# The first token block's plain tiles ahead of the second weight's block products, and its norm beside them

## The chip, the core and the metric

The kernel runs on one core of a Trainium2 chip. TensorE multiplies, VectorE and ScalarE work on elements, GpSimd (POOL) helps VectorE, and SyncE (SP) issues most transfers between DRAM and the on-chip memory. TensorE's results arrive in eight banks of 512 columns of fp32 (b0 to b7 in the rows). The metric is the time of one execution in microseconds (us), as the device reports it; lower is better.

## What is computed

One layer of a streaming encoder on 1088 tokens (1024 of a prompt, 64 of a running stream), width 1024, hidden width 2816:

```python
def _layer_norm(x, g, b):
    mu = x32.mean(-1, keepdims=True)
    var = jnp.square(x32 - mu).mean(-1, keepdims=True)
    return (x32 - mu) * lax.rsqrt(var + LN_EPS) * g + b

def _swiglu(x, wi, wo):
    a, u = jnp.split(x @ wi, 2, axis=-1)
    return (jax.nn.silu(a) * u) @ wo

h = _layer_norm(alpha * x + 0.5 * _swiglu(x, ffn1_wi, ffn1_wo), ln1_g, ln1_b)
oa, ob, ga, gb, states = mixer(h)          # z = h @ w_in, top-k attention with an indexer, band attention
mix = (jax.nn.sigmoid(ga) * ya + jax.nn.sigmoid(gb) * yb) @ w_out
h = _layer_norm(alpha * h + mix, ln2_g, ln2_b)
h = _layer_norm(alpha * h + 0.5 * _swiglu(h, ffn2_wi, ffn2_wo), ln3_g, ln3_b)
```

## The kernel before

Everything is fp32. An operand is split into a head and a rest, and a product is three matmuls: head with head, head with rest, rest with head. Data lie transposed: 8 tiles of 128 of the width (d or k), 22 hidden tiles of 128 (f), tokens along the columns. Tokens are cut twice: into blocks b of 384, 384 and 320 for the plain products and norms (`TB`), and into halves of 544 (`HT`), of two pieces of 272 (`SUB`) each, for the products by blocks.

**Order of the work.** `Plan` simulates all engines with a cost for each instruction while the program is written. TensorE's stream is written out in order; the other engines' work is put in as tasks with dependencies and priorities, and whenever TensorE's simulated clock passes a task's start, the task is written into its engine's queue. Tasks for TensorE (a norm's three matmul steps) come in at that point too, so the order on each engine is fixed when the program is built and isn't changed on the chip. While `st["solo"]` is set GpSimd gets no tasks. All instructions are recorded by one helper; so they all have line L120, and are told apart by tile.

**An FFN** is built by `add_ffn7`, for FFN1 (`gi` 0) and FFN2 (`gi` 2). The first weight's products are done in a scheme of seven block products. Of the hidden tiles, 0 to 17 (`KEPT_OUT` = 18) go out to DRAM and come back as tiles a, which are split into factors `fac`. The second weight is applied to these 18 in seven block products over 9 pairs, in the order P2, P1, P6, P5, P3, P7, P4 (`second`); each of the 63 units is 24 matmuls of 272 columns into eight banks (272 of the 512 columns are used), and after a product's ninth pair `take_out` adds the banks to the outputs y on VectorE. P2, P1 and P3 concern half 0 of the tokens, the others half 1. Hidden tiles 18 to 21 are multiplied plainly (`out_products`): six matmuls of 384 or 320 columns for two hidden tiles, one output tile d and one block b, and a VectorE instruction adds the bank to y. `early` does tiles 18 and 19 for d = 0, 1 and all blocks ahead of the block products (36 matmuls), `last_outputs` does the others behind them (252), block by block. The weights come through units: a raw chunk of 128 x 512 arrives (`wr` or `q`), ScalarE makes its head and VectorE its rest in a half of a tile `w_s`, in a rotation of four halves.

**The norms.** `add_up` adds the eight y of a block into `acc` while its outputs come. `layer_norm(b)`, called after block b, then consists of: a matmul of `acc` with ones (mean); eight centrings; eight squares, summed into `lns`; matmuls of `lns` with ones (variance, 1 column); the root on ScalarE and the reciprocal on VectorE (`rstd`); matmuls with `ident` that spread it over the partitions; eight scalings; and the output by `put`. In FFN1 `put` also splits the result into the tiles x that the projection z multiplies. In this text LN(b) is this norm of block b. In FFN1 LN(0) runs beside block 1's products, LN(1) beside block 2's and z's, LN(2) beside z's. In FFN2 the last block has its own form (`last_norm`), which sums most of the columns ahead (`sq`, `rest`).

The last part of z's first stretch makes the indexer's keys and queries, KH and QI. `split(hi, lo, src)` makes their heads by a ScalarE copy and their rests by a VectorE subtraction, both written directly into the queues.

Of the kernel before, what the change touches and what calls it, by code (L numbers as in the profile page):

```python
# [32 lines left out]
P = 128  # L33
# [306 lines left out]
def tile_trunk(ctx, tc, a):  # L340
# [12 lines left out]
    roles, turn = {}, {}  # L353

    def bank(role):
        banks = roles[role]
        i = turn.get(role, 0)
        turn[role] = i + 1
        t = banks[i % len(banks)]
        return psp.tile([P, 512], F32, name=f"b{t}", tag=f"b{t}")  # L360
# [180 lines left out]
    def layer_norm(b, Y, ACC, gi, tmp, put, room=None):  # L541
# [11 lines left out]
        t_mean = plan.task("pe", f"ln{b}", mean, [summed[b]], 1, ln_free, when=lambda: ln_free()[0])  # L553

        def copy(y):
            nc.scalar.activation(room[:, 0, :n], z[y][:, :n], AF.Copy)
            give(z[y])
# [42 lines left out]
        def var():  # L600
            p = take()
            for j, (c, m) in enumerate(toks):
                nc.tensor.matmul(p[:m, j:j + 1], z["s", 0][:, c:c + m], ones[:, :1], start=True, stop=True)
# [3 lines left out]
        def root():  # L607
# [3 lines left out]
            give(z["v"])  # L611
# [9 lines left out]
        t_var = plan.task("pe", f"ln{b}", var, [t_sum], 1, ln_free, when=lambda: ln_free()[0])  # L621
        t_root = plan.task("act", f"ln_r{b}", root, [t_var], 1)
        t_inv = plan.task("dve", f"ln_i{b}", inv, [t_root], 1)
        t_bc = plan.task("pe", f"ln{b}", spread, [t_inv], 1, ln_free, when=lambda: ln_free()[0])
# [8 lines left out]
        for k in range(KT):  # L633
            if room is None:
                t1 = plan.task("dve", f"ln_n{b}", lambda k=k: scale(k), [t_bc], 3)
            else:
# [188 lines left out]
    def add_up(ACC, Y, d, b, n, tmp):  # L825
# [6 lines left out]
        if d:  # L832
            summed[b] = plan.task(adders(n), "acc", add, [summed[b]] if d > 1 else (), 2, None, [Y[d, b]])
# [55 lines left out]
    def add_ffn7(wi, wo, wl, G, gi, put, beside_it, last, end):  # L889
# [10 lines left out]
        at, low, F, ACC, Y = Bag(), {}, {}, {}, {}  # L900
# [259 lines left out]
        def early():  # L1160

            f0 = KEPT_OUT
            wait(*(F[f].t[x, s] for f in (f0, f0 + 1) for x in ("h1", "h2") for s in range(2)))
# [1472 lines left out]
```

## Time and profile before

| | us |
|---|---|
| median of 3 runs | 2483.65 (2481.89 to 2483.95) |
| the profiled execution | 2481.9 |
| its span | 2480.1 |
| TensorE busy in the span | 2418.6 (98%) |
| VectorE busy | 1752.4 (71%) |
| ScalarE busy | 1298.7 (52%) |
| GpSimd busy | 343.8 (14%) |
| mean granted TensorE clock | 0.987 |

The profile shows one execution. A share of busy time is an average over parts of the program with different limits, so it says which engine bounds the whole and not what a certain place waits for. Windows cut the span into stretches and give each engine's busy time in them, and the clock that TensorE was granted (1.00 is its higher level of 2.4 GHz, 0.50 the lower of 1.2). The view in order of time gives, for an engine, runs of alike instructions, the idle time before each run, and the instruction that ended it. Starts in it count from the span's start. Some places: the first weight of FFN1 ends and the second begins at 492, P7 runs from 635.5 to 662.5, P4 to 689.5, the plain products to 733.5, then z; in FFN2 the second weight begins at 2200, and P7 and P4 run from 2345.5 to 2399.5.

### The profile page before, as it was taken

How to read it: one execution, taken by the hardware profiler on the slowest of the kernel's cores; microseconds unless marked ns; L12 is line 12 of the kernel's file. 1: busy time of each engine (PE TensorE's matmuls, PEld its weight loads, DVE VectorE, ACT ScalarE, POOL GpSimd, SP SyncE). 2: the span in 40 equal slices, each digit the busy share in tenths (PEclk: the TensorE clock that was granted, in tenths of full speed). 3: DMA queues.
4: the chain of work that ended last, by engine and by line, in shares of the span. 5: the costliest groups of instructions: out<-in, count | busy, mean ns of one | idle time of the engine just before them, and what ended most of it. 6: DMA issues, size and time to landing. Idle time of an engine off the chain costs nothing.

```text
span 2480.1 us, 46835 instructions
## 1 busy us (share of the span) xinstructions
PE 2418.6 (98%) x17338; PEld 2379.3 (96%) x17338; DVE 1752.4 (71%) x4244; ACT 1298.7 (52%) x2736; POOL 343.8 (14%) x459
## 2 busy tenths in 40 slices
PE   9999999999998999999999999999999999999996
PEld 8999999999998999999999998999999999999995
DVE  7666655667675889898776667679856655657758
ACT  5333333343334698878857777446533333334324
POOL 0000000000044222122253332311000000000004
PEclk9999999999998999999999999999999999999997
DMA  5466532263222322332221112555256643145322
GB/s 185 125 208 200 175 104 87 83 217 102 82 81 84 122 74 76 96 96 89 67 82 60 57 42 68 181 190 171 87 164 191 191 126 92 61 140 185 94 64 73
DMA packets 222357, 289.61 MB, mean 117 GB/s; under 512 B 20832, under 2 KB 146640, under 8 KB 222096
## 3 DMA queue, kind: packets, MB, share of 16 engines
q1 hardware_dynamic: 216080, 279.71, 36.4%
q10 hardware_dynamic: 5488, 4.70, 0.7%
q8 instruction: 136, 2.23, 0.4%
q0 software_dynamic: 560, 2.21, 0.2%
q14 instruction: 93, 0.76, 0.1%
HBM read 211.81 MB, written 75.00 MB: 116 GB/s over the span
## 4 chain that ended last, share of the span: by engine, by line
PE 84%; DVE 8%; DMA 2%; ACT 2%; issue 1%; POOL 1%; SPq 0%; DVEq 0%; ACTq 0%; POOLq 0%
PE b L120 84%; DVE y L120 1%; DVE w L120 1%; DVE scores L120 1%; DVE pt L120 1%; DMA ff_d<-c 1%; DVE w_s L120 0%; DVE mk L120 0%; DVE k L120 0%; DVE x L120 0%; DVE sc L120 0%; DMA st<-in_wo_dram 0%; ACT scores L120 0%; SPq L120 0%; DMA a<-ff_d 0%
## 5 line engine op out<-in xcount | busy, mean ns | idle before, releaser
L120 PE MATMUL b<-x,w_s 128*128 128x384 f32 (+1 forms) x3528 | 637.5, 332 | 7.7 <-DVE x L120 4.6
L120 PE MATMUL b<-A,w_s 128*128 128x272 f32 (+1 forms) x4824 | 632.2, 291 | 5.5 <-ACT w_s L120 2.3
L120 PEld LDWEIGHTS b<-A,w_s 128*128 128x128 f32 x4824 | 619.4, 189 | 9.3 <-ACT A L120 2.6
L120 PEld LDWEIGHTS b<-x,w_s 128*128 128x128 f32 x3528 | 587.1, 189 | 15.4 <-DVE x L120 6.4
L120 PE MATMUL b<-S,w_s 128*128 128x272 f32 x4032 | 516.8, 288 | 2.6 <-ACT c L120 2.6
L120 PEld LDWEIGHTS b<-S,w_s 128*128 128x128 f32 x4032 | 509.0, 188 | 5.6 <-ACT c L120 3.9
L120 ACT ACTIVATE w_s<-wr 128x512 fp32r<-128x512 f32 (+1 forms) x359 | 243.6, 679 | 358.4 <-PE b L120 197.6
L120 DVE TENSOR_TENSOR w_s<-wr,w_s 128x512 fp32r<-128x512 f32 (+1 forms) x335 | 245.3, 735 | 139.9 <-ACT w_s L120 135.1
L120 PE MATMUL b<-fac,w_s 128*128 128x272 f32 x1800 | 228.2, 288 | 1.3 <-DVE y L120 1.3
L120 PEld LDWEIGHTS b<-fac,w_s 128*128 128x128 f32 x1800 | 226.8, 188 | 1.5 <-ACT fac L120 1.5
L120 POOL TENSOR_TENSOR w_s<-wr,w_s 128x256 fp32r<-128x256 f32 x180 | 139.9, 805 | 321.7 <-ACT w_s L120 114.1
L120 ACT ACTIVATE c<-b 128x272 f32<-128x272 f32 (+1 forms) x262 | 102.1, 391 | 98.3 <-PE b L120 87.6
L120 DVE TENSOR_TENSOR c<-c,b 128x272 f32<-128x272 f32 x240 | 103.5, 434 | 62.9 <-PE b L120 59.1
L120 DVE TENSOR_TENSOR pt<-b,pt 128x512 fp32r<-128x512 f32 (+4 forms) x184 | 96.1, 545 | 22.6 <-ACT pt L120 21.0
L120 ACT ACTIVATE c<-c 128x272 f32<-128x272 f32 x160 | 68.8, 432 | 77.5 <-DVE c L120 75.0
L120 ACT ACTIVATE w<-w,mx 128x640 f32<-128x640 f32 (+5 forms) x144 | 100.4, 699 | 15.4 <-DVE mx L120 14.2
L120 POOL TENSOR_TENSOR w_i<-wr,w_i 128x256 fp32r<-128x256 f32 (+1 forms) x9 | 8.2, 928 | 693.0 <-ACT w_i L120 693.0
L120 ACT ACTIVATE fac<-a 128x544 fp32r<-128x544 f32 x73 | 48.0, 657 | 104.6 <-PE b L120 86.5
L120 PE MATMUL b<-pt,v 128*128 128x256 f32 (+3 forms) x672 | 97.5, 276 | 4.1 <-DVE o L120 2.1
L120 PEld LDWEIGHTS b<-pt,v 128*128 128x128 f32 (+1 forms) x672 | 93.5, 188 | 8.1 <-DVE pt L120 1.6
L120 ACT ACTIVATE w<-w,sm 128x640 f32<-128x640 f32 (+5 forms) x144 | 97.9, 700 | 5.0 <-DVE sm L120 4.2
L120 POOL TENSOR_TENSOR w_e<-wr,w_e 128x512 fp32r<-128x512 f32 x3 | 4.7, 1592 | 676.8 <-ACT w_e L120 676.8
(274 smaller groups left out, 3311.1 us busy)
## 6 DMA issues: line engine op xcount, KB each, us to landing
wr<-in_wi_dram SPq DMA_DIRECT2D x156, 256.0 KB, 3.1
ff_d<-c SPq DMA_DIRECT2D x144, 136.0 KB, 2.9
a<-ff_d SPq DMA_DIRECT2D x72, 272.0 KB, 3.6
st<-in_wo_dram SPq DMA_DIRECT2D x72, 256.0 KB, 5.1
tw_d<-st SPq DMA_DIRECT2D x72, 256.0 KB, 2.5
wr<-in_wz_dram SPq DMA_DIRECT2D x35, 512.0 KB, 3.6
wr<-tw_d SPq DMA_DIRECT2D x48, 256.0 KB, 2.7
wr<-in_wout_dram SPq DMA_DIRECT2D x24, 512.0 KB, 3.6
```

The lines of the kernel that those rows point to most:

```text
L120: r = real(*args, **kw)
```

## The change

In each FFN, `early` multiplies all four plain tiles for block 0 and all eight d (96 matmuls), with a weight unit for each d (`e0` to `e7`, chunks of 256 KB); it needs only the hidden tiles' half 0. ScalarE scales the 160 columns of y that belong to half 0 but not to block 0, and half 0's first `take_out` waits for that. Once P3 is out, `to_norm` opens pools for a norm, block 0 is summed, and `layer_norm(0)` is issued in P7's first unit. It uses the spare columns from 272 on of the eight product banks (`spare`): mean into b0 to b2, copied into a tile `room` by ScalarE; variance into b3; spread into b4 to b6, copied again. `last_outputs` does blocks 1 and 2, with all four tiles for each d. `split` becomes two tasks, the head on ScalarE or VectorE; a bank's next user waits until both are written. The pools of x are divided so that block 0's x can be made early. The core of the diff:

```diff
@@ split
-        nc.scalar.activation(hi, src, AF.Copy)
-        nc.vector.tensor_tensor(lo, src, hi.bitcast(F32), op=OP.subtract)
+        n = src.free_size()
+        t1 = plan.task((("act", 51 + 0.84 * n), ("dve", 69 + 1.04 * n)), "split", lambda e: (
+            nc.scalar.activation(hi, src, AF.Copy) if e == "act" else nc.vector.tensor_copy(hi, src)), (), 3, None, [src])
+        t2 = plan.task("dve", "split2", lambda: nc.vector.tensor_tensor(lo, src, hi.bitcast(F32), op=OP.subtract), [t1], 3)
+        readers.setdefault(roles["mm"][(turn["mm"] - 1) % len(roles["mm"])], []).extend([t1, t2])
@@ layer_norm
         def mean():
+            if spare:
+                for j, (c, m) in enumerate(toks):
+                    nc.tensor.matmul(spare[j][:, SUB:SUB + m], ones, ACC[b][:, c:c + m], start=False, stop=True,
+                                     skip_group_check=True)
+                return
...
         def copy(y):
+            if spare:
+                for j, (c, m) in enumerate(toks):
+                    nc.scalar.activation(room[:, 0, c:c + m], spare[j + 4 * (y == "b")][:, SUB:SUB + m], AF.Copy)
+                return
...
         def spread():
+            if spare:
+                for j, (c, m) in enumerate(toks):
+                    nc.tensor.matmul(spare[4 + j][:, SUB:SUB + m], z["r"][:m, j:j + 1].to_broadcast([m, P]),
+                                     ident[:m, :m], start=False, stop=True, skip_group_check=True)
+                return
@@ early
-            u = get_unit("o0", f0)
-            for d in (0, 1):
-                for b in range(3):
-                    out_products([f0, f0 + 1], d, b, u.slot, (d % 2) * 2)
-                touched.update((d, half, s) for half in range(2) for s in range(2))
-            done_with(u)
+            for d in range(KT):
+                u = get_unit(f"e{d}", NF)
+                out_products(fs, d, 0, u.slot, 0)
+                touched.update((d, 0, s) for s in range(2))
+                y = G.y[d][:, TB[0]:HT]
+                scaled[d] = plan.task("act", "f_z", lambda y=y: nc.scalar.activation(y, y, AF.Copy, scale=ALPHA), (), 2)
+                done_with(u)
@@ second
+            if final and x == "P3":
+                G.to_norm()
+                for d in range(KT):
+                    add_up(ACC, Y, d, 0, TB[0], G.early, [outs[d, 0, s, 0] for s in range(2)])
+            if x == "P7" and j == 0:
+                layer_norm(0, [Y[k, 0] for k in range(KT)], ACC, gi, G.early, put, G.early_room,
+                           [banks[t // 2, t % 2] for t in range(8)])
@@ last_outputs
+            norm_of(gi)(0)
             last()
             st["solo"] = False
...
-            for b in range(3):
-                if b:
+            for b in (1, 2):
+                if b > 1:
                     G.next_weights()
                 for d in range(KT):
...
-                    skip = 2 * (d < 2)
-                    out_products(fs[skip:], d, b, us[d].slot, skip)
+                    out_products(fs, d, b, us[d].slot, 0)
```

**In the order of instructions, first place:** TensorE in FFN1, from the first weight's last product to the second weight's first. Names are output bank, operands, columns, and count; A_101 holds the hidden tiles 20 and 21, h the tiles 18 and 19. Before:

```order
L120 MATMUL b_5009<-A_103,w_s_130 128x272 x12
L120 MATMUL b_5389<-h,w_s_129 128x384 x6
L120 MATMUL b_5404<-h,w_s_129 128x384 x6
L120 MATMUL b_5414<-h,w_s_129 128x320 x6
L120 MATMUL b_5424<-h,w_s_129 128x384 x6
L120 MATMUL b_5435<-h,w_s_129 128x384 x6
L120 MATMUL b_5446<-h,w_s_129 128x320 x6
L120 MATMUL b_5454<-fac_5379,w_s_129 128x272 x3
```

After, the last four of the eight units:

```order
L120 MATMUL b_5479<-h,w_s_129 128x384 x6
L120 MATMUL b_5479<-A_101,w_s_129 128x384 x6
L120 MATMUL b_5498<-h,w_s_129 128x384 x6
L120 MATMUL b_5498<-A_101,w_s_129 128x384 x6
L120 MATMUL b_5516<-h,w_s_130 128x384 x6
L120 MATMUL b_5516<-A_101,w_s_130 128x384 x6
L120 MATMUL b_5534<-h,w_s_130 128x384 x6
L120 MATMUL b_5534<-A_101,w_s_130 128x384 x6
L120 MATMUL b_5552<-fac_5380,w_s_129 128x272 x3
```

Between the two weights there are now 16 rows of six, all of 384 columns, each d with a unit of its own.

**Second place:** TensorE in P7 of FFN1, where the bank names of one unit follow each other in eight rows. Before, rows of products stand alone:

```order
L120 MATMUL b_6891<-fac_5383,w_s_130 128x272 x3
L120 MATMUL b_6895<-fac_5383,w_s_130 128x272 x3
L120 MATMUL b_6901<-fac_5383,w_s_130 128x272 x3
L120 MATMUL b_6906<-fac_5383,w_s_130 128x272 x3
L120 MATMUL b_6910<-fac_5383,w_s_130 128x272 x3
```

After, about the same place with LN(0)'s spread (three matmuls with `ident`) in it:

```order
L120 MATMUL b_6989<-fac_5384,w_s_130 128x272 x3
L120 MATMUL b_6995<-fac_5384,w_s_130 128x272 x3
L120 MATMUL b_6999<-fac_5384,w_s_130 128x272 x3
L120 MATMUL b_6999<-ident,rstd 128x128
L120 MATMUL b_7005<-ident,rstd 128x128
L120 MATMUL b_7010<-ident,rstd 128x128
L120 MATMUL b_7005<-fac_5384,w_s_130 128x272 x3
L120 MATMUL b_7010<-fac_5384,w_s_130 128x272 x3
L120 MATMUL b_7014<-fac_5384,w_s_130 128x272 x3
```

The spread goes to the banks of the products around it, and the next products into two of them come right behind.

**Third place:** TensorE in z of FFN1, around LN(1)'s variance (`ones,lns`) and spread (`ident,rstd`). x_0 is block 0's x. Before:

```order
L120 MATMUL b_7996<-x_0_7853,w_i_7895 128x384 x3
L120 MATMUL b_8040<-x_0_7738,w_i_7896 128x384 x3
L120 MATMUL b_8044<-ones,lns_7907 128x1 x3
L120 MATMUL b_8040<-x_0_7758,w_i_7896 128x384 x3
L120 MATMUL b_8040<-x_0_7771,w_i_7896 128x384 x3
L120 MATMUL b_8040<-x_0_7821,w_i_7896 128x384 x3
L120 MATMUL b_8040<-x_0_7835,w_i_7896 128x384 x3
L120 MATMUL b_8077<-ident,rstd 128x128 x3
L120 MATMUL b_8040<-x_0_7841,w_i_7896 128x384 x3
```

After, from the last plain products of block 2 on:

```order
L120 MATMUL b_7921<-A_101,w_e 128x320 x6
L120 MATMUL b_7955<-x_0_7390,w_s_7835 128x384 x3
L120 MATMUL b_7955<-x_0_7426,w_s_7835 128x384 x3
L120 MATMUL b_7955<-x_0_7428,w_s_7835 128x384 x3
L120 MATMUL b_7955<-x_0_7439,w_s_7835 128x384 x3
L120 MATMUL b_7955<-x_0_7451,w_s_7835 128x384 x3
L120 MATMUL b_7974<-ones,lns_7804 128x1 x3
L120 MATMUL b_7979<-acc,ones 128x320
L120 MATMUL b_7955<-x_0_7457,w_s_7835 128x384 x3
L120 MATMUL b_7955<-x_0_7463,w_s_7835 128x384 x3
L120 MATMUL b_7955<-x_0_7468,w_s_7835 128x384 x3
L120 MATMUL b_8006<-ident,rstd 128x128 x3
```

LN(1)'s variance stood behind 26 rows of z's products and stands behind five now. LN(2)'s mean (`acc,ones`) came after z's first row and now comes after LN(1)'s variance.

## Rows read from the trace of the kernel before

**Rows 1.** The page, busy us, share of the span and instructions of each engine:
```profile
PE 2418.6 (98%) x17338; PEld 2379.3 (96%) x17338; DVE 1752.4 (71%) x4244; ACT 1298.7 (52%) x2736; POOL 343.8 (14%) x459
```

**Rows 2.** Windows of 40 us: us, busy of each engine, granted clock, DMA share, GB/s:
```profile
720.00:760.00 40.00, 35.65 (x199) 34.24 (x197) 32.66 (x62) 21.67 (x43) 25.53 (x28) 0.91 0.31 97
760.00:800.00 40.00, 32.97 (x176) 31.48 (x176) 21.20 (x48) 18.48 (x43) 13.45 (x12) 0.83 0.25 87
2440.00:2480.00 40.00, 16.02 (x97) 14.65 (x95) 29.78 (x53) 16.94 (x34) 19.12 (x18) 0.61 0.32 112
```

**Rows 3.** TensorE in order, end of FFN1: start, us, instructions, wait before and releaser:
```profile
736.36 0.78 PE L120 MATMUL b<-acc,ones 128*128 128x320 f32 x2 [2.17 <-DVE acc L120]
...
751.99 1.15 PE L120 MATMUL b<-ones,lns 128*128 128x1 f32 x6 [2.19 <-DVE lns L120]
...
756.98 0.84 PE L120 MATMUL b<-ident,rstd 128*128 128x128 f32 x3
...
763.14 0.69 PE L120 MATMUL b<-x,w_s 128*128 128x384 f32 x1 [3.10 <-DVE x L120]
764.95 2.93 PE L120 MATMUL b<-x,w_s 128*128 128x384 f32 x8 [1.12 <-DVE x L120]
770.68 1.28 PE L120 MATMUL b<-ones,lns 128*128 128x1 f32 x6 [2.80 <-DVE lns L120]
```

**Rows 4.** Windows of 5 us, behind FFN1 and behind FFN2's start of the second weight:
```profile
750.00:755.00 5.00, 3.01 (x12) 3.04 (x13) 4.36 (x11) 2.43 (x7) 2.65 (x4) 0.73 0.31 84
755.00:760.00 5.00, 5.00 (x19) 4.62 (x18) 2.93 (x7) 1.00 (x3) 3.17 (x4) 0.59 0.08 26
765.00:770.00 5.00, 2.87 (x8) 2.36 (x8) 3.44 (x7) 0.14 (x1) 5.00 (x3) 0.50 0.25 92
770.00:775.00 5.00, 4.32 (x16) 4.22 (x17) 0.83 (x3) 0.40 (x2) 0.18 (x1) 0.50 0.00 0
2210.00:2215.00 5.00, 5.00 (x30) 5.00 (x30) 1.67 (x4) 1.18 (x2) 0.00 (x0) 0.68 0.49 164
```

**Rows 5.** TensorE in order, starts of the second weight in FFN1, then FFN2:
```profile
492.11 6.15 PE L120 MATMUL b<-h,w_s 128*128 128x384 f32 x36
499.56 3.63 PE L120 MATMUL b<-fac,w_s 128*128 128x272 f32 x27 [1.31 <-DVE y L120]
...
2209.08 5.14 PE L120 MATMUL b<-A,w_s 128*128 128x272 f32 x27 [2.30 <-ACT w_s L120]
```

**Rows 6.** Windows of the last two block products of FFN1, P7 and P4:
```profile
635.50:662.50 27.00, 27.00 (x218) 27.00 (x217) 18.06 (x33) 9.96 (x17) 0.00 (x0) 1.00 0.31 89
662.50:689.50 27.00, 27.00 (x218) 27.00 (x217) 12.62 (x24) 8.43 (x14) 0.00 (x0) 1.00 0.23 73
```

**Rows 7.** VectorE at FFN1's end, in order; the last one a group of 720 to 760:
```profile
738.16 2.87 DVE L120 TENSOR_TENSOR y<-y,b 128x384 f32<-128x384 f32 x6
...
744.94 0.55 DVE L120 TENSOR_TENSOR KH<-b,KH 64x384 fp32r<-64x384 f32 x1 [2.21 <-ACT KH L120]
...
757.87 4.29 DVE L120 SCALAR_TENSOR_TENSOR y<-y,lnp,b 128x384 f32<-128x384 f32 x8 [2.07 <-PE b L120]
...
L120 DVE TENSOR_TENSOR x<-y,x 128x384 fp32r<-128x384 f32 x5 | 4.3, 877 | 0.0
```

**Rows 8.** The page's groups, whole program: a weight unit's head and rest, mean ns:
```profile
L120 ACT ACTIVATE w_s<-wr 128x512 fp32r<-128x512 f32 (+1 forms) x359 | 243.6, 679 | 358.4 <-PE b L120 197.6
L120 DVE TENSOR_TENSOR w_s<-wr,w_s 128x512 fp32r<-128x512 f32 (+1 forms) x335 | 245.3, 735 | 139.9 <-ACT w_s L120 135.1
```

**Rows 9.** All engines in order, end of the program:
```profile
2446.88 3.71 POOL L120 TENSOR_TENSOR y<-y,c 128x384 f32<-128x384 f32 x3
...
2451.96 1.20 PE L120 MATMUL b<-ones,rest 128*80 128x1 f32 x8 [6.17 <-DVE rest L120]
...
2462.16 8.91 DVE L120 TENSOR_TENSOR y<-y,c 128x320 f32<-128x320 f32 x11
```

More of the change, by code (lines that the diff above doesn't have):

```diff
@@ L359, in bank @@
         t = banks[i % len(banks)]
+        for x in readers.pop(t, ()):
+            plan.until(lambda: x.end is not None)
         return psp.tile([P, 512], F32, name=f"b{t}", tag=f"b{t}")
@@ L539, in combine, with layer_norm @@
         of(e).tensor_tensor(y[:, :n], y[:, :n], x[:, :n], op=op)
-    def layer_norm(b, Y, ACC, gi, tmp, put, room=None):
+    def layer_norm(b, Y, ACC, gi, tmp, put, room=None, spare=None):
         n = TB[b]
@@ L600, in var @@
         def var():
-            p = take()
+            p = spare[3][:, SUB:] if spare else take()
             for j, (c, m) in enumerate(toks):
-                nc.tensor.matmul(p[:m, j:j + 1], z["s", 0][:, c:c + m], ones[:, :1], start=True, stop=True)
+                nc.tensor.matmul(p[:m, j:j + 1], z["s", 0][:, c:c + m], ones[:, :1], start=not spare, stop=True,
+                                 skip_group_check=bool(spare))
             z["v"] = p
@@ L610, in root @@
                 nc.scalar.activation(r[:m, c], z["v"][:m, c], AF.Sqrt, bias=epst[:m])
-            give(z["v"])
+            if not spare:
+                give(z["v"])
         def inv():
@@ L1160, in early @@
         def early():
-            f0 = KEPT_OUT
-            wait(*(F[f].t[x, s] for f in (f0, f0 + 1) for x in ("h1", "h2") for s in range(2)))
+            fs = list(range(KEPT_OUT, NF))
+            wait(*(F[f].t["h1", s] for f in fs for s in range(2)))
             wait(*G.sums_made)
@@ L1267, in take_out @@
                 wait(*G.read[d])
+            elif not half:
+                wait(scaled[d])
             def go():
@@ L1278, in last_outputs @@
         def last_outputs():
-            fs = list(range(NF - 4, NF))
-            wait(*(F[f].t[x, s] for f in fs for x in ("h1", "h2") for s in range(2)))
+            fs = list(range(KEPT_OUT, NF))
+            wait(*(F[f].t["h2", s] for f in fs for s in range(2)))
+            norm_of(gi)(0)
             last()
@@ L1349, in add_ffn7 @@
                 elif x == "early":
-                    want.append((("o0", f), lambda q: q.rearrange("p (d c) -> p d c", d=2), wog[:, :2, f * P:(f + 2) * P]))
-                    unit("o0", f)
+                    for d in range(KT):
+                        want.append(((f"e{d}", NF), lambda q: q, wl[d // 2][:, d % 2 * 512:(d % 2 + 1) * 512]))
+                        unit(f"e{d}", NF)
                     steps.append(early)
@@ L1439, in ring_tile, with second_tiles, early_norm @@
         G.ring = pool(open_(name), name, side).tile([P, 2, 2, NT], F32R, name="h")
-    def second_tiles(G, p, n):
-        G.a = {(x, j): p.tile([P, HT], F32, name=f"a{x}_{j}") for x in ("12", "11", "21", "22") for j in range(KEPT_OUT // 2)}
+    def second_tiles(G, p, p2, n):
+        G.a = {(x, j): (p2 if x in ("12", "21") else p).tile([P, HT], F32, name=f"a{x}_{j}")
+               for x in ("12", "11", "21", "22") for j in range(KEPT_OUT // 2)}
         return [p.tile([P, 2, HT], F32R, name=f"fac{i}") for i in range(n)]
+    def early_norm(G, side):
+        G.early = pool(open_("early"), "early", side)
+        G.early_room = G.early.tile([P, 1, 384], F32, name="room")
     p1 = stage_tiles(G1, "top1", None)
@@ L2407, in to_out @@
         plan.until(lambda: all(t.end is not None for t in gated.values()))
+        close("x12")
         close("x")
@@ L2484, in to_second2, with to_norm2 @@
         close("s")
-        G2.fac = [G2.xc["A12"][:, k] for k in range(4)] + second_tiles(G2, pool(open_("s"), "back2"), 1)
+        p = pool(open_("s"), "back2")
+        G2.fac = [G2.xc["A12"][:, k] for k in range(4)] + second_tiles(G2, p, pool(open_("back"), "back2b"), 1)
+    def to_norm2():
+        close("back")
+        early_norm(G2, None)
+    G2.to_norm = to_norm2
     common(G2)
@@ L2505, in last_of_ffn2 @@
     def last_of_ffn2():
+        close("early")
         close("s")
```

42 lines of the change are left out of this document (27 added, 15 removed).

## The prediction

> **What bounds the kernel now.** First I read the busy shares of the span: TensorE is busy for 2418.6 of 2480.1 us [rows 1], so nearly all of the time is matmuls, and the change takes none away. What it can win lies in the 61.5 us in which TensorE is idle and in the stretches where it runs at the lower of its two clocks. Then I read the 40 us windows, to see where these are. Three places hold most: the end of FFN1 with the start of the projection z (720 to 800: 35.65 and 32.97 busy, granted clock 0.91 and 0.83) and the end of the program (2440 to 2480: 16.02 busy) [rows 2], and the two places where the second weight's products begin (rows below).
>
> At the end of FFN1 TensorE's own order in time shows five waits, all for VectorE: 2.17 (the sum for LN(2)'s mean), 2.19 (LN(1)'s sum of squares), 3.10 and 1.12 (x of block 1), 2.80 (LN(2)'s sum of squares), together 11.4 us [rows 3]. LN(b) is the norm of token block b. After the first waits the clock falls: 3.01 us at 0.73, 5.00 at 0.59, 2.87 at 0.50, 4.32 at 0.50 [rows 4]. Work of B us at share c of the full clock would take B·c, so 0.8 + 2.0 + 1.4 + 2.2 = 6.5 us are lost to the clock. The place costs 17.9 us.
>
> The reason is VectorE. The three norms come one after another behind the last products; while TensorE multiplies blocks 1 and 2, VectorE still has LN(0), and LN(1) and LN(2) come late. Two more things slow it: an instruction `x<-y,x` of 384 columns takes 0.88 us there, where six of the form `y<-y,b` went by in 2.87, 0.48 each, and it stands 2.21 us before KH's rest until ScalarE has copied KH's head [rows 7].
>
> At the starts of the second weight TensorE waits 1.31 us in FFN1 (for y) and 2.30 in FFN2 (for a weight unit from ScalarE) [rows 5], and behind the latter 5.00 us run at 0.68 [rows 4], another 1.6 us: 5.2 us in all.
>
> **Part 1: the plain tiles of block 0 go ahead.** Matmuls: before 36 + 252, after 96 + 192 per FFN, the same 288, and of the same widths. So TensorE's work is equal. Before, the 36 last 6.15 us [rows 5] for 24 × 384 + 12 × 320 = 13,056 columns, 0.47 ns each; 96 of 384 columns last 17.4 us. In these 17 us the first factors are split and the first weight units of the block products prepared, for which there were 6 us. The late unit (2.30) and the clock behind it should go, the wait on y too. What is added there: 8 weight units instead of one, that is 7 loads of 256 KB on SP's queue, 7 heads on ScalarE at 0.68 and 7 rests on VectorE at 0.74 [rows 8], and per unit one ScalarE scaling of 160 columns (no row of its own; at most the 0.68 of 512 columns). VectorE there has 8 rests (5.9), 8 outputs (0.54 as the scalings of the same width [rows 7], 4.3) and 5 factor rests (544 columns, about 0.74 too, 3.7): 13.9 of 17.4 us, so it fits, without much room. A unit is used up in 2.2 us where a block product's unit lasts 3.0. Four halves of a weight tile rotate, so each has some 6 us from its last use to its next; that covers 0.68 + 0.74 and the handovers. I take −4 of the 5.2, with −1 to −5.2 as ends. What is queued behind a late load on SP is the return of the factors from DRAM, for which the first block product would wait.
>
> **Part 2: LN(0) beside P7 and P4.** Half 0 of the tokens is complete with P3, so block 0's sum and norm can run beside the last two block products, 54 us of unbroken TensorE work in which VectorE is busy 18.06 + 12.62 = 30.7 us and GpSimd 0 [rows 6]. FFN2's two windows read the same. LN(0) adds to VectorE: 22 additions and subtractions (7 sum, 8 centre, 7 squares) at 2.87/6 = 0.48, 8 scalings at 4.29/8 = 0.54, 8 of the bias at most 0.48 [rows 7]: 10.6 + 4.3 + 3.8 = 18.7 us. Then it is busy 49.4 of 54, 91%, where there was 57%. ScalarE has 18.4 of 54 us busy [rows 6], so its 8 squares and six copies fit.
>
> Does TensorE wait there? Three ways. The mean, the variance and the spread sit in its queue at fixed places; if VectorE is late, everything behind waits. By the order the mean comes 35 product rows (13 us) into P7, and the variance 33 product rows (12.4 us) on; the 15 TT between them make 7.2 us, beside the outputs and factors which come anyway: just enough. Between variance and spread there are nine product rows (3.4 us); in the FFN1 end of before 4.99 us lay between the two, with no wait shown at the spread [rows 3]. So 0 to 1.4 us here. And the banks: LN(0) writes into the spare columns of the eight product banks, so the next product into such a bank waits until ScalarE has copied or read it. After the spread the product into b6 comes one row (0.37 us) later, while three copies of 128 columns have to end, each at most 0.68 [rows 8]: 0.3 to 1.7 us. For two norms I take 2 × (0.6 + 0.9) = +3; the ends are 0 and +8 (two late sums of 2 us, as the 2.19 and 2.80 of now, on top).
>
> A rule speaks against this place. The rows show banks of the norm and of products apart (the mean and variance of LN(1) and LN(2) wait for VectorE only) [rows 3]. The Trainium skill, "PSUM — Partial Sum Buffer", section "PSUM bank collisions raise a hardware error", states that two engines may not touch one bank's same partitions at once, whatever the columns. By it the 2 × 0.9 us of bank waits are in the sum, which is −22 below; if a product could go on beside a reader of other columns, it would be −24. No run of before shows it.
>
> **Part 3: what then is left at the end of FFN1.** Only blocks 1 and 2 are multiplied there (192 matmuls, about 30 us), with LN(1) beside block 2. LN(1)'s variance stood behind 26 rows of z, now behind five; LN(1) starts with a VectorE that hasn't LN(0) to do. From its mean to its variance TensorE has 81 matmuls of 320 columns and 15 of 384, at 0.47 ns a column 14.9 us; VectorE has 15 TT of LN(1), 8 outputs and 7 sums of block 2: 30 × 0.48 = 14.4 us, less what GpSimd takes. That is tight, so not all is won. KH's and QI's heads as tasks take the 2.21 us out of VectorE's way too. LN(2)'s spread comes after x of block 1 is in use. I leave 3 us of the 17.9 standing: −15, between −18 and −9.
>
> **Part 4: the end of the program.** The last product ends at 2451.96 − 6.17 = 2445.8; after it TensorE waits 6.17 us for `rest`, the chain of LN(2) runs to 2462.2 [rows 9], and the span ends at 2480.1, 34.3 us behind the product. In the 6.17 us VectorE has, by the order, the last output and six more instructions up to the last `rest`, 0.88 us each, while GpSimd centres columns of LN(1) (`y<-y,c`) [rows 9]. In the new order it is the output and six as well, but LN(1)'s centres are done before: 7 × 0.48 = 3.4 instead of 6.2 us, −2.8. From the last reciprocal on VectorE has 19 instructions where it had 24: 5 × 0.48 = 2.4, and of block 1's columns only the scaling and bias are left. I take −5 to −6, with −6 in the sum, from −3 to −10. Block 0's output leaves beside P4, before the tail.
>
> **Part 5: the rest** costs nothing I can find. `split()` as tasks moves KH's and QI's heads between ScalarE and VectorE, 12 short copies. TensorE's order from z on through the mixer is the same, and so are its waits there.
>
> **The sum.** −4 − 15 − 6 + 3 = −22, made against the profiled run of 2481.9 us (span 2480.1 and 1.8 around it): 2459.9. The median of the three runs is 1.75 above the profiled run, so **2461.7 us**. The ends added: −1 − 9 − 3 + 8 = −5 and −5.2 − 18 − 10 = −33; not all fall to one side at once.
>
> **The rivals.** *A: VectorE is too full beside P7 and P4.* At 91% every unforeseen 0.1 us on its 60 instructions there is late for the variance. Then both norms stall TensorE two or three times by 2 to 2.8 us, as at FFN1's end now [rows 3], +6 per norm instead of 1.5: 2461.7 + 9 = 2471. For it speaks that 0.88 us is paid where 0.48 is due [rows 7]; against it that GpSimd is idle there [rows 6], and those 0.88 are in a stretch where it works. A page says the same of the mechanism, in a sentence that the rest doesn't need: the Trainium skill, "SBUF — State Buffer", section "Who interferes with whom", has a two-input VectorE instruction contend with GpSimd's reads; by it the lateness in A would fall away with GpSimd idle and the sum be nearer −23, while by the 0.88 alone it is −13.
>
> *B: the end of FFN1 stays late.* LN(1) and LN(2) keep their waits of 2.19 and 2.80, x of block 1 its 1.12, with 3 or 4 us of clock: 10 of 17.9 stay instead of 3: 2469. For it speaks the tight 14.4 against 14.9.
>
> *C: nothing of it arrives*, since loads or weight units limit the early block: 8 units in 17 us, each in one of four slots. A unit late by 1 us each time costs 8 per FFN, 16 in all, and with part 1's gain gone 20: 2482, no change.
>
> *D, the slower side: the clock falls in the middle of P7 and P4.* Now it is 1.00 in both [rows 6]. If VectorE is late at mean, variance and spread of both norms so that the clock goes to half as at 765 to 775 [rows 4], 10 us of work at half clock lose 5 us per place on top of some 3 of wait: 6 places × 8 = 48, against 25 won: 2484 + 23 = 2507. It decides from about four such places on; the 1.31 us wait in FFN1 had no such fall behind it: the next 27 products took 3.63 us, 0.13 each, as in P7 (218 in 27.00) [rows 5, 6].
>
> **Chances.** Forecast 0.58 (its own range 2453 to 2467), A 0.17, B 0.17, C 0.04, D 0.04. A measurement of this kernel tells apart about 0.2%, 5 us. Faster by more than that: forecast, A and B, 0.92; within it 0.04; slower 0.04. The range from 2451 to 2474 takes in the forecast's own and the middles of A and B.
>
> **What would show it.** Right: 36 → 96 matmuls before the block products and no wait over 1 us behind them; windows of P7 and P4 with VectorE at about 25 and 24 of 27 and TensorE at 26 or more; 720 to 800 with 76 or more busy instead of 68.6 at clock 1.00; the wait before `rest` 3 us in place of 6. Wrong: TensorE waits on `lns` or on ScalarE within P7 over 2 us each (A), five waits as before at z (B), waits on w_s in the early block (C), a granted clock under 0.9 in P7 or P4 (D).

## The result, and the profile after

The median went from 2482.77 to 2456.05 us (2454.63 to 2459.75): a ratio of 0.9901 with a 95% interval of 0.9886 to 0.9916, so 1% or 25 us faster by the ratio (the two medians lie 26.7 us apart). The forecast was 2461.7, with a range from 2451 to 2474. The profiled execution took 2455.64 us.

TensorE's busy time has fallen by 8 us though it has the same products, and the clock accounts for that (0.992 on average instead of 0.987); the rest of the 26.3 us by which the span is shorter is waits. The page's busy line, against [rows 1]:

```profile
PE 2410.4 (98%) x17352; PEld 2375.3 (97%) x17352; DVE 1764.0 (72%) x4284; ACT 1303.0 (53%) x2760; POOL 316.6 (13%) x437
```

Windows of 40 us, and two of 5 us behind FFN1 (columns as in [rows 2] and [rows 4]):

```profile
720.00:760.00 40.00, 37.47 (x225) 36.95 (x224) 34.58 (x68) 21.10 (x43) 23.82 (x27) 0.96 0.34 104
760.00:800.00 40.00, 38.12 (x219) 36.04 (x218) 24.12 (x51) 17.69 (x47) 10.53 (x14) 0.93 0.24 77
755.00:760.00 5.00, 2.69 (x11) 2.69 (x12) 3.90 (x11) 1.64 (x5) 0.00 (x0) 0.67 0.09 20
760.00:765.00 5.00, 5.00 (x21) 4.46 (x20) 2.47 (x6) 1.89 (x5) 0.43 (x1) 0.64 0.09 31
```

At the end of FFN1 TensorE was busy for 68.6 of 80 us at 0.91 and 0.83 of the clock [rows 2]; it is busy for 75.6 at 0.96 and 0.93. Of the five waits of [rows 3] one is left, for LN(2)'s sum of squares, and a new one stands 40 us later in the indexer's scores. TensorE in order:

```profile
757.31 1.28 PE L120 MATMUL b<-ones,lns 128*128 128x1 f32 x6 [2.53 <-DVE lns L120]
...
797.28 0.91 PE L120 MATMUL b<-KH,QI 128*128 128x512 f32 x2 [1.88 <-ACT rl L120]
```

The 5 us windows show what a wait of 2.53 us costs besides itself: 2.69 us of work at 0.67 and 5.00 at 0.64, 0.9 + 1.8 = 2.7 us. Behind the 1.88 it was 3.12 us at 0.77 and 5.00 at 0.89 (795 to 805), 1.3 us.

The starts of the second weight, first of FFN1, then of FFN2, against [rows 5]: no wait in the first, 0.74 in the second, and no lowered clock.

```profile
490.05 1.21 PE L120 MATMUL b<-h,w_s 128*128 128x384 f32 x6
...
506.85 18.36 PE L120 MATMUL b<-fac,w_s 128*128 128x272 f32 x145
```

```profile
2185.70 1.21 PE L120 MATMUL b<-h,w_s 128*128 128x384 f32 x6
...
2203.44 12.27 PE L120 MATMUL b<-A,w_s 128*128 128x272 f32 x96 [0.74 <-DVE y L120]
```

P7 and P4 of FFN1, against [rows 6]: VectorE is busy for 26.95 of 27.2 us in P7 and for 20.2 of 27 in P4, and TensorE loses 0.54 us.

```profile
645.20:672.40 27.20, 27.20 (x221) 27.20 (x220) 26.95 (x54) 16.55 (x31) 0.00 (x0) 1.00 0.32 95
672.40:699.40 27.00, 26.46 (x212) 26.25 (x211) 20.23 (x41) 13.10 (x27) 0.00 (x0) 1.00 0.39 121
```

That 0.54 is behind LN(0)'s spread (`ident,rstd`). TensorE in order, and ScalarE's copies out of the banks:

```profile
672.74 0.83 PE L120 MATMUL b<-ident,rstd 128*128 128x128 f32 x6
673.33 0.63 PE L120 MATMUL b<-fac,w_s 128*128 128x272 f32 x3
674.49 25.13 PE L120 MATMUL b<-fac,w_s 128*128 128x272 f32 x198 [0.54 <-ACT room L120]
```

```profile
673.16 0.28 ACT L120 ACTIVATE room<-b 128x128 f32<-128x128 f32 x1 [1.03 <-PE b L120]
673.99 0.45 ACT L120 ACTIVATE room<-b 128x128 f32<-128x128 f32 x2 [0.55 <-PE b L120]
```

The spread went into b4, b5 and b6. The product into b5 came next, so the copy out of b5 waited for it, and the product into b6 waited for the copies. FFN2 has the same 0.54.

The end of the program, against [rows 9]: TensorE's last products and the chain of LN(2), then VectorE:

```profile
2427.27 1.04 PE L120 MATMUL b<-A,w_e 128*128 128x320 f32 x6
...
2430.19 0.54 PE L120 MATMUL b<-ident,rstd 128*128 128x128 f32 x3 [1.32 <-DVE rstd L120]
2433.41 1.23 PE L120 MATMUL b<-ones,rest 128*80 128x1 f32 x8 [2.67 <-DVE rest L120]
```

```profile
2441.75 6.50 DVE L120 TENSOR_TENSOR y<-y,c 128x320 f32<-128x320 f32 x11 [1.16 <-ACT c L120]
...
2449.69 0.79 DVE L120 TENSOR_SCALAR y<-y,lnp 128x320 f32<-128x320 f32 x2
```

The wait before `rest` is 2.67 instead of 6.17 us, the chain from there to the first `y<-y,c` of block 2 takes 8.3 instead of 10.2, and from that to the span's end it is 12.1 instead of 17.9.

Cut at places that both traces have, the 26.3 us come from five stretches:

| stretch | before | after | difference |
|---|---|---|---|
| to the first plain product ahead of FFN1's second weight | 492.1 | 490.1 | −2.1 |
| from there to the first product of z | 241.4 | 240.9 | −0.5 |
| z, mixer and FFN2's first weight | 1467.1 | 1454.7 | −12.4 |
| FFN2's second weight, to the last plain product's end | 245.2 | 242.6 | −2.6 |
| from there to the span's end | 34.3 | 25.5 | −8.8 |

The first line isn't the change's. Up to there the fourteen kernels of this document have the same instructions in the same order on each engine, but for the last weight unit, and their profiled executions took from 489.3 to 492.1 us. What moves them is open. The granted clock between 10 and 20 us varied too, 0.75 in before, 0.87 in after and from 0.74 to 1.00 in the others, but it doesn't order the times: five executions at 1.00 took 490.6 to 491.3.

### The profile page after: what moved, and what is told of

Same layout as the page of the kernel before. It is cut to its first block, busy times and chain, and to the rows that moved or that the text cites. A ratio compares the mean times of both kernels' runs of the same rounds, so it can differ in the third digit from the quotient of the medians.

```text
span 2453.8 us, 46965 instructions
## 1 busy us (share of the span) xinstructions
PE 2410.4 (98%) x17352; PEld 2375.3 (97%) x17352; DVE 1764.0 (72%) x4284; ACT 1303.0 (53%) x2760; POOL 316.6 (13%) x437
## 3 DMA queue, kind: packets, MB, share of 16 engines
q0 software_dynamic: 560, 2.21, 0.2%
## 4 chain that ended last, share of the span: by engine, by line
PE 86%; DVE 8%; DMA 2%; ACT 2%; issue 1%; POOL 0%; SPq 0%; DVEq 0%; ACTq 0%; POOLq 0%
PE b L120 86%; DVE y L120 1%; DVE w L120 1%; DVE scores L120 1%; DVE pt L120 1%; DVE x L120 1%; DVE sc L120 0%; DVE k L120 0%; DVE w_s L120 0%; DMA st<-in_wo_dram 0%; DVE mk L120 0%; DMA sc_d<-sc 0%; DMA x<-o_d 0%; ACT w L120 0%; DMA z<-in_ckT_dram 0%
## 5 line engine op out<-in xcount | busy, mean ns | idle before, releaser
L120 PE MATMUL b<-A,w_s 128*128 128x272 f32 (+2 forms) x4872 | 639.3, 290 | 2.2 <-ACT A L120 0.8
L120 ACT ACTIVATE w_s<-wr 128x512 fp32r<-128x512 f32 (+1 forms) x370 | 250.0, 677 | 372.7 <-PE b L120 213.1
L120 DVE TENSOR_TENSOR w_s<-wr,w_s 128x512 fp32r<-128x512 f32 (+1 forms) x347 | 252.0, 728 | 141.4 <-ACT w_s L120 135.9
L120 ACT ACTIVATE c<-b 128x272 f32<-128x272 f32 x260 | 101.0, 390 | 96.6 <-PE b L120 90.0
L120 PE MATMUL b<-m,w_s 128*128 128x384 f32 (+1 forms) x576 | 98.1, 330 | 0.6 <-DVE w_s L120 0.6
L120 PEld LDWEIGHTS b<-m,w_s 128*128 128x128 f32 x576 | 95.8, 188 | 1.5 <-DVE w_s L120 1.0
```

What stands on the lines that cost most here:

```text
L120: r = real(*args, **kw)
```

## The experiments

All times are medians; each run's ratio is to runs of the kernel before on its own chip.

### Each FFN alone

The change in one FFN (`NEWS` is `(0,)` or `(2,)`); the other has its plain tiles and its norm where before had them.

```diff
+NEWS = (0,)
...
+            if gi not in NEWS:
+                u = get_unit("o0", f0)
...
```

> The change in FFN1 alone, FFN2 as before. Theory: the gain is local, so it is what the trace of after shows of FFN1: 0.5 us at the start of its second weight and 12.3 us at its end and the start of z, 12.8 in all, about 2470 us, with the end of FFN2 as before (6 us wait for rest). Rival 1: the 2.1 us that after was ahead at the first weight's end come from the change too: 2468. Rival 2: some of the gain is given back later in the mixer, 2474 or more.

> The change in FFN2 alone, FFN1 as before. Theory: 2.6 us at its second weight's stretch and 8.8 us at the end of the program, 11.4 in all, about 2471 us; the five waits at FFN1's end stay (11 us). With FFN1 alone the two gains add up to 24. Rival: the gains hang together (FFN1's end moves the mixer's work), so that the two don't add: sum under 20 or over 28.

Measured: 2462.33 us, ratio 0.9922 (0.9910 to 0.9934), and 2461.57, ratio 0.9918 (0.9905 to 0.9932). Each alone gains some 20 us, together they gain 25. That the parts add up, as expected, is wrong. The end of the program behaves as forecast, with the wait for `rest` in the first as before and in the second as after:

```profile
2434.35 1.20 PE L120 MATMUL b<-ones,rest 128*80 128x1 f32 x8 [6.15 <-DVE rest L120]
```

```profile
2439.33 1.23 PE L120 MATMUL b<-ones,rest 128*80 128x1 f32 x8 [2.68 <-DVE rest L120]
```

But at FFN1's end, whose order was that of before in the second run, the waits were 6.1 us where they are 11.4 in [rows 3]. What both runs share is what I had kept in both: the heads and rests of KH and QI as tasks, and the divided pools.

The traces show where the parts overlap. The stretch from z's first product to the first of the indexer's scores lasts 71.8 us in before, 57.9 with FFN1 alone, 61.0 with FFN2 alone and 57.6 with both: most of the gain there comes twice. So does that of FFN2's second weight, 245.2 us in before, 242.1 in either run and 242.6 in after. In the first run FFN2 has the order of before, and TensorE waits 0.39 us at the start of that weight where it waited 2.30 in [rows 5]:

```profile
2193.33 11.93 PE L120 MATMUL b<-A,w_s 128*128 128x272 f32 x93 [0.39 <-DVE y L120]
```

Only the end of the program goes with FFN2's part alone: 34.3 us behind the last product in before, 34.4 in the first run, 26.0 in the second, 25.5 in after.

### The tasks alone, and the pools alone

Before's order, with the new `split` and the new pools; then the same with the old `split`:

```diff
-NEWS = (0,)
+NEWS = ()
@@ split (in the second run only)
+        nc.scalar.activation(hi, src, AF.Copy)
+        nc.vector.tensor_tensor(lo, src, hi.bitcast(F32), op=OP.subtract)
```

> Before's order of all products and norms, with KH's and QI's heads and rests as tasks and with the divided pools of the change. The change in FFN2 alone came out at 2461.6, 9 us less than its own part, and its trace shows FFN1's end, whose order is that of before, with 6 us of waits instead of 11. Theory: the tasks do this by themselves, so this is 9 to 12 us under before, 2470 to 2473. Rival: it is run to run, or the pools: 2479 or more (the pools are told apart by the next run).

> As the last, with heads and rests written directly as in before: only the pools of the change. Theory: the waits at FFN1's end come back (11 us and the low clock); at most the wait for a weight unit at FFN2's second weight is gone, 3 us: 2479 to 2482. Rival (the pools free memory earlier, and that is the 9 us): 2470 to 2473.

Measured: 2469.81 us, ratio 0.9955 (0.9943 to 0.9968), and 2479.30, ratio 0.9992 (0.9983 to 1.0001). Tasks and pools together are worth 11 us in the old order, the pools by themselves 2, which can't be told from zero; so the tasks are worth 9 to 11. TensorE at the end of FFN1, first with the tasks, then without:

```profile
733.73 0.78 PE L120 MATMUL b<-acc,ones 128*128 128x320 f32 x2 [1.58 <-DVE acc L120]
...
744.99 0.83 PE L120 MATMUL b<-ones,lns 128*128 128x1 f32 x6 [1.00 <-POOL lns L120]
...
753.88 0.45 PE L120 MATMUL b<-x,w_s 128*128 128x384 f32 x1 [0.82 <-DVE x L120]
755.54 1.33 PE L120 MATMUL b<-x,w_s 128*128 128x384 f32 x6 [1.22 <-POOL x L120]
...
761.26 0.78 PE L120 MATMUL b<-ones,lns 128*128 128x1 f32 x6 [1.16 <-DVE lns L120]
```

```profile
735.59 0.78 PE L120 MATMUL b<-acc,ones 128*128 128x320 f32 x2 [1.58 <-DVE acc L120]
...
751.22 0.80 PE L120 MATMUL b<-ones,lns 128*128 128x1 f32 x6 [2.17 <-DVE lns L120]
...
761.42 0.44 PE L120 MATMUL b<-x,w_s 128*128 128x384 f32 x1 [3.75 <-DVE x L120]
...
768.96 0.88 PE L120 MATMUL b<-ones,lns 128*128 128x1 f32 x6 [2.81 <-DVE lns L120]
```

Without them the waits are those of [rows 3]. VectorE with them, to be set against KH's rest in [rows 7], which stood 2.21 us for ScalarE:

```profile
741.06 0.55 DVE L120 CAST KH<-b 64x384 fp32r<-64x384 f32 x1 [0.50 <-ACT KIW L120]
...
742.16 1.11 DVE L120 TENSOR_TENSOR KH<-b,KH 64x384 fp32r<-64x384 f32 x2
```

A rest that is written directly stands in VectorE's queue from the moment its product is recorded; VectorE stands there until the product is done and ScalarE has made the head, with LN(1)'s centrings and sums behind it. In before it stood 3.3 us in this way (2.21, 0.55 and 0.55) ahead of LN(1)'s last sum, for which TensorE waited until 751.99 [rows 3]:

```profile
746.60 1.35 DVE L120 TENSOR_TENSOR y<-y,b 128x384 f32<-128x384 f32 x3
...
750.86 0.98 DVE L120 TENSOR_TENSOR lns<-lns,lns 128x384 f32<-128x384 f32 x1
```

As a task a rest comes when its head is there. In the old order LN(1)'s variance needs those sums, so TensorE waits, the clock falls, and x of block 1 is late as well. A task also lets VectorE make a head, as it did with KH's first; no run tells how much of the 9 to 11 us is the place in the queue and how much the choice of engine.

### The norm behind P4 again, with the tasks and without

Block 0's plain tiles stay ahead. Its sum and its norm go from `second` back to `last_outputs`, the place behind P4, and the wait there for the finished norm (`norm_of`) goes:

```diff
-            if x == "P7" and j == 0:
-                layer_norm(0, ...)
-            norm_of(gi)(0)
             last()
+            for d in range(KT):
+                add_up(ACC, Y, d, 0, TB[0], G.tmp, ...)
+            layer_norm(0, [Y[k, 0] for k in range(KT)], ACC, gi, G.tmp, put, ...)
```

> Block 0's four plain tiles stay ahead of the block products, but its sum and its norm come behind P4, beside block 1's products, as in before. Theory (VectorE's place for LN(0) is what wins at the two ends): the second weight's starts keep their 4 us, but at FFN1's end three norms now hide beside two blocks' products instead of three, so its waits come back, 12 to 20 us more than in after, and the end of FFN2 5 to 9 us: 2473 to 2485. Rival (it is enough that fewer plain products stand behind P4): under 2462.

> Block 0's plain tiles ahead, its norm behind P4, and heads and rests written directly. Theory: the norm's place and the tasks each relieve VectorE at FFN1's end, and either is enough there: with the early norm the tasks were worth nothing (2455 without them), without it they are worth 8 us or so: 2473 to 2478, with four or five waits for VectorE at z. Rival: the tasks are worth the same little here, 2467 as with them.

> After, with KH's and QI's heads and rests written directly as in before and not as tasks. Theory: a small part, 0 to 3 us: 2456 to 2459, with VectorE's wait for KH's head back at z's start. Rival: these tasks are what frees VectorE for LN(1) and LN(2), 5 us or more: 2461 or more.

Measured: 2467.19 us, ratio 0.9943 (0.9930 to 0.9955), with the tasks; 2472.09, ratio 0.9963 (0.9951 to 0.9975), without; and after with heads and rests written directly: 2454.94, ratio 0.9893 (0.9878 to 0.9909). By ratios, in us of 2482.8, each good to 3 or 4 us:

| order | written directly | as tasks |
|---|---|---|
| before's | 0 (pools −2) | −11 |
| plain tiles ahead, norm behind P4 | −9 | −14 |
| plain tiles and norm ahead (the change) | −27 | −25 |

Down the left column the tiles ahead give 9 and the norm 17 more; down the right one 3 and 10. Across, the tasks give some 10, then 5, then nothing. Only the first of these differs clearly from the last. The traces show the same for the stretch from z's first product to the scores: written directly 71.8 us (69.4 with the pools), 67.1 and 55.3 down the column, as tasks 61.0, 61.4 and 57.6. So the early norm and the tasks are two remedies for one wait: with LN(0) out of the way LN(1)'s variance comes ahead of KH, and there is nothing behind KH's rest for which TensorE waits. In the run with both norm ahead and heads written directly the one wait left at z was shorter even than in after, 1.38 us, and the 1.88 us in the indexer's scores was gone (no wait over 0.26 there):

```profile
757.69 0.88 PE L120 MATMUL b<-ones,lns 128*128 128x1 f32 x6 [1.38 <-DVE lns L120]
```

My figure for the late norm with tasks, 2473 to 2485, was too high: it took the waits at FFN1's end to come back in full. From the start of z to 775 us they are 6.5 us with tasks and 7.9 without, of the 11.4 in [rows 3]; without tasks they are mainly four, of 2.52, 1.67, 1.50 and 1.85 us, for VectorE as I expected but for the 1.67, which is for GpSimd. The end of the program came back in part. With the late norm the stretch from the first matmul on `rest` to the span's end was 28.2 us (2437.18 to 2465.4), 28.1 in before, and 20.4 in after. But the wait before `rest` was 3.34 and not the 6.17 of [rows 9], so that this part of the gain needs only the tiles ahead:

```profile
2437.18 1.20 PE L120 MATMUL b<-ones,rest 128*80 128x1 f32 x8 [3.34 <-DVE rest L120]
```

### Is VectorE really full beside P7?

Eight additions on VectorE for each of the two norms, which the planner's costs don't count:

```diff
         def both(e):
+            if spare:
+                for _ in range(8):
+                    tc.nc.vector.tensor_tensor(ln["more"][:, :n], z["s", 1][:, :n], z["s", 1][:, :n], op=OP.add)
             of(e).tensor_tensor(z["s", 0][:, :n], z["s", 0][:, :n], z["s", 1][:, :n], op=OP.add)
```

> After, with eight additions of 384 columns (0.48 us each, into a tile that nobody reads) on VectorE ahead of LN(0)'s last sum of squares, in both FFNs; the planner doesn't know of them, so the order is after's. Theory: VectorE has no idle time in P7 (26.95 of 27.2 us busy) and the variance's place in TensorE's order leaves no slack, so TensorE waits some 3.5 us at each variance, and up to 2 us go to the clock: 2462 to 2467. Rival: there is slack, since work is pulled ahead as soon as it can be: within 1.5 of 2456.

Measured: 2472.37 us, ratio 0.9960 (0.9947 to 0.9973): 15 us more than after by the ratios, 16 by the medians, and above the 2462 to 2467 that I expected. VectorE's eight instructions, TensorE at the variance, and the two windows there:

```profile
667.94 4.71 DVE L605 TENSOR_TENSOR more<-lns 128x384 f32<-128x384 f32 x8
```

```profile
673.17 1.44 PE L120 MATMUL b<-ones,lns 128*128 128x1 f32 x6 [4.30 <-DVE lns L120]
```

```profile
670.00:675.00 5.00, 1.83 (x8) 1.83 (x9) 4.37 (x10) 0.00 (x0) 0.00 (x0) 0.66 0.00 0
675.00:680.00 5.00, 5.00 (x30) 5.00 (x29) 4.31 (x10) 1.44 (x3) 0.00 (x0) 0.65 0.26 68
```

4.71 us on VectorE became a wait of 4.30 on TensorE, and 1.83 us at 0.66 and 5.00 at 0.65 cost 2.4 more: 6.7 us per norm, 13.4 in all; FFN2's wait was 4.28. The additions took 0.59 us each, not the 0.48 I had reckoned, which is part of my miss. There is hardly any slack: of what VectorE is late there, TensorE pays all but 0.4 us, and the clock adds half. (The profiled execution, at 2476.07 us the slowest of six, is 7 us longer than after's in each of the two stretches with a norm and 6.5 in the mixer, where I could tie no place to the change.) In after this bill doesn't come: the planner writes the variance into TensorE's order where VectorE will be done, and its costs hold there. That they hold because GpSimd is idle beside P7 is my reading and not tested.

### Three of the waits that are left

LN(0)'s spread into the places of banks that the products reach last (on top of heads written directly):

```diff
+                far = sorted(range(3, 8), key=lambda t: (t - ln["at"] - 1) % 8)[2:]
-                    nc.tensor.matmul(spare[4 + j][:, SUB:SUB + m], ...
+                    nc.tensor.matmul(spare[t][:, SUB + off:SUB + off + m], ...
```

> After with heads and rests written directly (2454.9 by itself) and with LN(0)'s spread put into the three spare bank places that the products reach last, with room in b3 beside the variance. In after ScalarE's copies from b5 and b6 had to wait for the product into b5, and the product into b6 waited 0.54 us for them, in both FFNs. Theory: these two waits go or shrink under 0.2, 1 us in all, 2453 to 2455. Rival: the product into b7, two rows on, waits as long instead: no difference.

Measured: 2451.97 us, ratio 0.9887 (0.9872 to 0.9902). The 1 us can't be told by the time, but by the trace, in both FFNs. In FFN1 the spread, and then 99 products without a wait:

```profile
672.01 0.83 PE L120 MATMUL b<-ident,rstd 128*128 128x128 f32 x6
672.59 12.66 PE L120 MATMUL b<-fac,w_s 128*128 128x272 f32 x99
```

LN(2)'s variance later in TensorE's order:

```diff
+        if gi == 0 and b == 2:
+            t_var.lead = 3500
```

> After, with the variance of LN(2) in FFN1 written into TensorE's order as if it were ready 3.1 us later: behind six more rows of z's products. In after TensorE waits 2.53 us there for VectorE's sum of squares, and some 2.7 us go to the low clock behind it. Theory: VectorE's chain isn't faster by it, and x of block 2, which is finished just when z asks for it (773 us), is late by what TensorE has gained: no gain, within 2 us of 2456, with a wait for x in place of that for lns. Rival: the wait and the clock are gained, 2451.

Measured: 2450.96 us, ratio 0.9886 (0.9870 to 0.9903). My theory fell. The wait is gone, no wait for x came in its place, and the clock stayed at 1.00 throughout; the products of block 2 in z start 4.9 us earlier (768.15 against 773.01):

```profile
758.27 0.71 PE L120 MATMUL b<-ones,lns 128*128 128x1 f32 x6
...
761.20 0.63 PE L120 MATMUL b<-ident,rstd 128*128 128x128 f32 x3
...
768.15 7.21 PE L120 MATMUL b<-x,w_s 128*128 128x320 f32 x48
```

The reason is in after's trace, on VectorE: it stood 3.00 us itself, for the spread that TensorE did late, being at 0.64 of the clock after its own wait.

```profile
762.53 3.75 DVE L120 SCALAR_TENSOR_TENSOR y<-y,lnp,b 128x320 f32<-128x320 f32 x8 [3.00 <-PE b L120]
```

So VectorE's chain was slowed by TensorE's wait, which I had taken for its consequence only. This is in the trace; the median's 5 us less than after are inside the two intervals.

x's rests in FFN1 on VectorE alone:

```diff
-            return plan.task(adders(n), f"ln_q{b}", lo, [t1], 3)
+            return plan.task((("dve", 69 + 1.04 * n),), f"ln_q{b}", lo, [t1], 3)
```

> After, with the rests of x in FFN1 on VectorE alone. In after VectorE's four casts x<-y took 0.91 us each while GpSimd made three rests, and one took 0.35 beside an idle GpSimd. Theory: VectorE gives 3 x 0.5 us for the rests and gets back 4 x 0.56 on the casts, so LN(2)'s sum comes 0.7 us or so earlier and its wait is under 2 us in place of 2.53: 2454 to 2456. Rival: the casts are slow for another reason, and VectorE has just 1.5 us more: the wait grows to 4 us and the clock stays down longer, 2458 or more.

Measured: 2452.02 us, ratio 0.9894 (0.9879 to 0.9908), no difference by the time. VectorE and GpSimd in after, then VectorE and TensorE here:

```profile
743.93 3.65 DVE L120 CAST x<-y 128x384 fp32r<-128x384 f32 x4
```

```profile
743.90 2.10 POOL L120 TENSOR_TENSOR x<-y,x 128x384 fp32r<-128x384 f32 x2
```

```profile
744.90 1.15 DVE L120 CAST x<-y 128x384 fp32r<-128x384 f32 x4
```

```profile
756.81 0.78 PE L120 MATMUL b<-ones,lns 128*128 128x1 f32 x6 [1.05 <-DVE lns L120]
```

Four casts take 1.15 us instead of 3.65, and LN(2)'s wait is 1.05 instead of 2.53, as expected. Some 1.5 us still went to the clock behind it (3.95 us at 0.77 and 5.00 at 0.89).

### The three edits together

Heads written directly, the far bank places, and the later variance.

> After with three edits that showed a shorter wait each: heads and rests written directly, LN(0)'s spread in the bank places that the products reach last, and LN(2)'s variance six rows later. Theory: what is won adds up where the places differ: the two waits at the spreads (1.1 us), and at LN(2)'s variance the 1.4 us wait and the clock behind it, since x of block 2 isn't late by it: 2447 to 2451 by the medians so far, with no wait over 0.3 us from the second weight of FFN1 to the indexer's scores. Rival: with the heads written directly VectorE is behind at x of block 2, and the wait moves there: 2452 or more.

Measured: 2451.01 us, ratio 0.9875 (0.9859 to 0.9892). It is the lowest ratio of all, but its interval touches after's (0.9886 to 0.9916), so that it beats after is likely and not shown. My "no wait over 0.3 us" didn't hold, for a wait did move, a small one, to x of block 2:

```profile
770.57 5.86 PE L120 MATMUL b<-x,w_s 128*128 128x320 f32 x38 [0.64 <-DVE x L120]
```

## Why the prediction was right, point by point

The sum was −22 against the profiled run, the traces show −26.3, of which 2.1 lie ahead of the change. The sign, the size and most places were right; one reason was wrong.

**Part 1, −4.** Right in size, in FFN2 by luck: the wait of 1.31 is gone, that of 2.30 is 0.74, and the 1.6 us of clock are back, 4.5 us. The early block took 16.8 us (490.05 to 506.85; 17.4 reckoned) with no wait on a weight unit. But the 3.2 us at FFN2's start are not shown to come from the tiles ahead: with the old order there and new pools the wait was for y, 2.01, 1.83 and 0.39 us in three runs, with the clock at 1.00 behind it in all three, and the run with 0.39 spent no longer on that weight than after. In FFN1 the old order waited 0.86 to 2.50 us in four runs and the tiles ahead never, so some 1 to 2 us of the part are theirs.

**Part 2, +3.** 1.1 us, both at the banks; the term was mis-sized. Neither mean nor variance was late, although VectorE was nearer to its limit in P7 (99%) than the 91% over both products that I had reckoned; over both it was 87%. I had let its lateness depend on its share. What decides is whether the planner's costs hold, since TensorE's steps are written where VectorE is reckoned to be done. The doubt behind rival A was sound: 4.71 us more than the planner knew cost 6.7. The bank rule of the Trainium skill ("PSUM — Partial Sum Buffer", section "PSUM bank collisions raise a hardware error") showed itself as guard waits, between ScalarE's copy and a product into other columns of the bank: 0.54 us, at the low end of my 0.3 to 1.7. These waits are the program's own guards; no run lets a reader and a product meet in one bank.

**Part 3, −15.** 12.4 us in that stretch: 14.2 up to the indexer's first score, less 1.8 behind it. One of the five waits stayed, with its clock (2.53 + 2.7), where I had left 3 us in all; and 1.88 us with 1.3 of clock came in the indexer's scores. The mechanism was right: with heads and rests written directly the tiles and the norm ahead take the stretch from z to the scores from 69.4 to 55.3 us. But beside the tasks the same change of order takes it only from 61.0 to 57.6, so most of the 12.4 could have been had by the tasks alone. The likelihood of B, that some of FFN1's waits stay, was thus partly borne out, for LN(2) and not for LN(1).

**Part 4, −6.** 8.8 us. The step on `rest` was right in its wait (2.67 against 3.4 reckoned), which doesn't need the early norm (3.34 without it), but not in its gain: LN(1)'s variance and spread now stand ahead of it, with 1.32 us of wait, so that from the last product to `rest` it is only 1.1 us less. The gain is in what I had put at 2.4: from block 2's first `y<-y,c` on 5.9 us, since eleven of these go by in 6.50 instead of 8.91 us and none of block 1's columns follow; and 1.9 in the chain. Without the early norm all of the 7.8 us from `rest` on are lost.

**Part 5, nothing.** The wrong step. "`split()` as tasks moves KH's and QI's heads" was reckoned at no gain beyond the 2.21 us of VectorE's wait in part 3. Alone it is worth 9 to 11 us, most of FFN1's end. That the forecast didn't suffer is luck: in this change it is worth nothing, since the early norm takes the same waits away. Nor are the waits behind z the same, as I had it: the wait in the scores, 1.88 us in after and 1.33 to 1.60 in the four other runs with the early norm in FFN1 and the tasks, is 0.26, 0.26 and 0.79 in the three with the early norm and without them. I had read the 2.21 us as a share of VectorE's load; it is a wait at the head of a queue with LN(1) behind it.

Rivals A, C and D didn't come: neither norm waited for VectorE beside P7, the loads and weight units kept up, and the clock was 1.00 in P7 and P4. The 0.88 us on which A rested belongs to GpSimd's company: with x's rests on VectorE alone six `x<-y,x` took 2.90 us, 0.48 each. The hidden load showed the mechanism of D at two places of six, at 6.7 us each against the 8 that I had put.

## What to carry to other kernels

Two parts of a change that relieve the same wait don't add up, and neither can be priced with the other in place: take each alone, and both away, before a gain is put down to one of them. An instruction written into an engine's queue ahead of its input costs the wait of all that stands behind it, not its own. And where a scheduler fixes the order with modelled costs, an engine that was 99% busy beside a matmul stream did no harm while the model held; 4.7 us that the model didn't know were paid with 4.3 of wait and 2.4 of clock.

## What the runs showed of the hardware that I had not expected

- VectorE's cast `x<-y` of 384 columns took 0.91 us on average while GpSimd worked on `x<-y,x`, and 0.29 without GpSimd on these (3.65 and 1.15 for four). The Trainium skill ("SBUF — State Buffer", section "Who interferes with whom") says that a cast on VectorE may take the pair of ports that it shares with GpSimd, and that the other then stands still; these rows agree.
- A single wait of TensorE of 2.53 or 4.30 us was followed by 5 us windows at 0.64 to 0.67 of the clock, 2.4 to 2.7 us lost each time; a wait of 0.54 or 0.74 was not. In between its length alone didn't decide: behind 1.05 us (LN(2)'s variance, x's rests on VectorE) and 1.88 us (the scores in after) the clock fell to 0.77 and 0.89, behind 1.83 and 2.01 us (FFN2's second weight in the old order, new pools) it stayed at 1.00.
- The granted clock in the first 20 us of the program differs between executions, 0.74 to 1.00 between 10 and 20 us, and the first 490 us by up to 3 us. The clock there doesn't explain the 3 us: with 0.87 it was 490.1, with 1.00 490.6 to 491.3.
